# Eight middle taps of a depthwise convolution as products with diagonals on TensorE

## The chip, the cores and the metric

The kernel runs on one core of a Trainium2 chip. The metric is the device time of one execution in microseconds (us). The core has five instruction streams, named here as the profile names them: PE (TensorE; PEld is its weight load), DVE (VectorE), ACT (ScalarE), POOL (GpSimd) and SP (SyncE, which issues the DMA transfers).

## The reference

Two transformer-like blocks run one after the other on 256 tokens of width 1024. The change lies in the first. In each of its two layers half of the channels of the input projection go through a gated convolution over time, the other half through a recurrence (`wkv_scan`) that reads a matrix state. Cut to what matters here:

```python
def conformer_conv(u, conv_w, conv_b, cnorm_g, cnorm_b):
    val, gate = jnp.split(u, 2, axis=-1)
    z = val * jax.nn.sigmoid(gate)
    z = dwconv(z, conv_w) + conv_b          # 31 taps, one filter per channel, 512 channels
    z = group_norm(z, CONV_GROUPS, cnorm_g, cnorm_b, LN_EPS)
    return jax.nn.silu(z)

for l in range(2):
    mod_x = silu(c) @ ada_w[l] + ada_b[l]
    mod_c = silu(c_ctx) @ ada_w[l] + ada_b[l]
...
    yc, s_f, s_b = rwkv_scans(prep_c, s_zero, s_zero, emit=not last)
    prep_x = rwkv_prep(ux[..., CONV_IN:], *rw)
    yx, _, _ = rwkv_scans(prep_x, s_f, s_b, emit=True)
    mix_x = jnp.concatenate([conformer_conv(ux[..., :CONV_IN], *cv), rwkv_out(yx, prep_x, *post)], axis=-1)
    x = x + gt1 * (mix_x @ w_out[l])
    x = x + gt2 * swiglu(modulate(rmsnorm(x, norm2_g[l]), sh2, sc2), ffn_wg[l], ffn_wu[l], ffn_wd[l])
```

There are three such convolutions: on the context in layer 0, on x in layer 0 and on x in layer 1.

## The kernel before, in words

Channels lie on partitions, 128 at a time, and the 256 tokens along the free axis; the 512 channels of a convolution are four feature tiles. The instructions of all stages are written out in Python as generators and then ordered for each engine by a scheduler that follows a modelled timeline, so that the order on an engine isn't the order of the code. Each engine runs its own order strictly in turn.

Two of the convolutions, those of the context in layer 0 and of x in layer 1, run inside `wide` (L1425), the stretches A and B below. `wide` runs the recurrence of that layer (`rwkv`). While that waits, it asks `filler` (L1427) for pieces of other work for TensorE. The filler first gives `conv_in` (L659): per feature tile two weight transfers, the products `pb<-xf,wh` and `pb<-xf,wl`, a sigmoid, and the gate on VectorE (L670), which leaves z in `self.x[0]`. Then it gives `ada_steps` (L478): the modulation vector, as fp32 products of raw weights with 32 columns (`pb<-raw,csil`), in groups of four that lie side by side in TensorE's array, a small product that turns the row (`pb<-const,T2b`), and an addition on VectorE (L503). Almost all products have line L333, the helper `mm`.

The recurrence needs the inverse of small triangular matrices. `inverse` (L944) does it by a recursion of 31 steps on VectorE, a product (L962) and a subtraction (L964) each; the last subtraction is `self.inverted`. Behind it come two 32x32-block transposes on VectorE (L967 into `qt`, L969 into `qc`), products of 32 columns on TensorE, and the writes of the matrix Q on VectorE and ScalarE (the last of them L1011 on VectorE, in the trace as `S<-acc` and `S<-ps` of 32x512). From Q on the sequential `chain` (L1075) can start; its first product is `acc<-Sb,S`. Beside this stand `gram` products whose results VectorE masks (L1029, L1065) and transposes on TensorE (L1035, L1052).

The convolution itself is `conv` (L700). In `wide` its 31 taps are split by their distance from the centre. VectorE takes the centre tap with the bias (L719) and 19 more (L726), each one instruction `T1c += w * z` over a shifted slice. GpSimd takes the 11 outer ones in two instructions each, a product into `tap` (L732) and an addition into the accumulator `acc`, that is `self.x[1]` (L733), which it first sets to zero (L720), and at the end adds VectorE's sum (L737). VectorE's first instruction is tied behind `self.inverted` by `issue_after`, so the taps don't delay the recursion. GpSimd isn't tied. The group norm of `conv` (products `acc<-x,const`) follows, then `mixed_in`.

The third convolution (`hold=True`, x in layer 0) runs on GpSimd alone, in the background of the feed-forward stage. Raw weights pass through a ring of four 512 KB buffers (`raw`, L345), filled by DMAs on SP's queue in the order in which the program asks for them; the filler's products have two PSUM buffers (`pb`).

Of the kernel before, what the change touches and what calls it, by code (L numbers as in the profile page):

```python
# [14 lines left out]
P = 128  # L15
D = 1024
NF = 8
T = 256
# [19 lines left out]
NPOOL, NPOOLE, NPOOLC = (11, 0), (11, 0), (30, 0)  # L38
# [129 lines left out]
def _layout(a):  # L168
# [40 lines left out]
    for l in range(2):  # L209
# [9 lines left out]
        f[f"wo{l}"] = (n["w_out"][l].reshape(NF, P, D))  # L219
        lo = np.zeros((P, 2, 1024), np.float32)  # L220
# [35 lines left out]
EVAC1 = [x for f in range(8) for x in (("DA"[f // 2 % 2 == 0], "e", f), ("A", "h", f), ("P" if f in (4, 5) else "D", "l", f))]  # L256


class Prog:
# [440 lines left out]
    def conv(self, l, z, acc, npool, hold=False):  # L700
# [4 lines left out]
        taps = sorted((j for j in range(31) if j != 15), key=lambda j: abs(j - 15))  # L705
        nv, na = 30 - npool[0] - npool[1], npool[1]
        parts = [("v", taps[:nv]), ("a", taps[nv : nv + na]), ("p", taps[nv + na :])]

        order = []
        for k, js in parts:  # L710
            order += [((i + 0.5) / len(js), k, j) for i, j in enumerate(js)]
        order.sort()
        zc = [acc[:, f, :] for f in range(4)]
        for f in range(4):
            w = lambda j: self.cols[:, o + 4 * j + f : o + 4 * j + f + 1]
            av = self.T1([P, T]) if nv else None
            if nv:
                with self.tc.issue_after(self.inverted.ins):
                    nc.vector.tensor_scalar(av, z[:, f, :], w(15), self.col(f"convb{l}", f), ALU.mult, ALU.add)  # L719
                nc.gpsimd.memset(zc[f], 0.0)  # L720
            else:
                nc.gpsimd.tensor_scalar(zc[f], z[:, f, :], w(15), None, ALU.mult)
            for i, (_, k, j) in enumerate(order):
                d, s = slice(max(0, 15 - j), min(T, T + 15 - j)), slice(max(0, j - 15), min(T, T + j - 15))
                if k == "v":
                    nc.vector.scalar_tensor_tensor(av[:, d], z[:, f, s], w(j), av[:, d], ALU.mult, ALU.add)  # L726
                else:
                    t = self.t(self.pool, [P, T], "tap", bufs=NTAP)
                    if k == "a":
                        nc.scalar.mul(t[:, d], z[:, f, s], w(j))  # L730
                    else:
                        nc.gpsimd.tensor_scalar(t[:, d], z[:, f, s], w(j), None, ALU.mult)  # L732
                    nc.gpsimd.tensor_add(zc[f][:, d], zc[f][:, d], t[:, d])  # L733
                if i % 5 == 4:
                    yield
            if nv:
# [902 lines left out]
```

## Time and profile before

| | us |
|---|---|
| median of 3 runs (lowest, highest) | 2769.9 (2768.45, 2772.62) |
| profiled execution, its own time | 2769.65 |
| its span in the profile | 2767.9 |
| mean granted clock of TensorE | 0.963 |
| busy: TensorE, weight loads | 2618.3, 2278.6 |
| busy: VectorE, ScalarE, GpSimd | 1734.4, 1310.6, 622.5 |
| stretch A, first `wide` (context, layer 0) | about 112 to 316 |
| stretch B, second `wide` (x, layer 1) | about 1107 to 1325 |

Times in the trace are counted from the start of the span. Engines work side by side, so busy times overlap. A granted clock of 1.00 is 2.4 GHz and of 0.50 is 1.2 GHz; a value between them is a mean over a stretch that had both. A row of a timeline groups equal instructions that follow one another; its duration is from the first start to the last end, and the bracket behind it says how long the engine was idle before and what released it.

### The profile page before, as it was taken

How to read it: one execution, taken by the hardware profiler on the slowest of the kernel's cores; microseconds unless marked ns; L12 is line 12 of the kernel's file. 1: busy time of each engine (PE TensorE's matmuls, PEld its weight loads, DVE VectorE, ACT ScalarE, POOL GpSimd, SP SyncE). 2: the span in 40 equal slices, each digit the busy share in tenths (PEclk: the TensorE clock that was granted, in tenths of full speed). 3: DMA queues.
4: the chain of work that ended last, by engine and by line, in shares of the span. 5: the costliest groups of instructions: out<-in, count | busy, mean ns of one | idle time of the engine just before them, and what ended most of it. 6: DMA issues, size and time to landing. Idle time of an engine off the chain costs nothing.

```text
span 2767.9 us, 53680 instructions
## 1 busy us (share of the span) xinstructions
PE 2618.3 (95%) x22398; PEld 2278.6 (82%) x22398; DVE 1734.4 (63%) x2747; ACT 1310.6 (47%) x1984; POOL 622.5 (22%) x609
## 2 busy tenths in 40 slices
PE   7889988999889998899899899999999999999998
PEld 4857867888678897856799899789899898889897
DVE  3895778654577555996555655666655655656655
ACT  5523553434565346423544544644544544644543
POOL 0293999920130001392100000010000000100000
PEclk8989999999999999989999999999999999999999
DMA  7344424434423354253455555524555554525653
GB/s 251 102 153 168 142 97 153 142 127 142 156 77 115 130 180 148 102 184 108 145 184 188 192 187 186 186 77 161 186 186 183 186 187 168 171 77 183 207 188 116
DMA packets 118768, 430.71 MB, mean 156 GB/s; under 512 B 13174, under 2 KB 13686, under 8 KB 118524
## 3 DMA queue, kind: packets, MB, share of 16 engines
q1 hardware_dynamic: 118524, 427.28, 44.6%
q8 instruction: 175, 2.87, 0.4%
q14 instruction: 69, 0.57, 0.1%
HBM read 425.13 MB, written 2.10 MB: 154 GB/s over the span
## 4 chain that ended last, share of the span: by engine, by line
PE 79%; DVE 12%; ACT 5%; issue 2%; DMA 2%; POOL 1%; SPq 0%; ACTq 0%; DVEq 0%; POOLq 0%
PE pb L333 33%; PE acc L333 25%; PE ps L333 19%; DVE wl L342 3%; DVE T L962 1%; DVE S L964 1%; DMA raw<-in_ada 1%; ACT wh L341 1%; PE acc L438 0%; DVE acc L619 0%; ACT L384 0%; DVE T1c L726 0%; DVE x L620 0%; DMA raw<-in_wr 0%; DVE S L1029 0%
## 5 line engine op out<-in xcount | busy, mean ns | idle before, releaser
L342 DVE TENSOR_TENSOR wl<-raw,wh 128x1024 fp32r<-128x1024 f32 (+1 forms) x654 | 812.8, 1246 | 618.6 <-ACT wh L341 388.1
L341 ACT CAST wh<-raw 128x1024 fp32r<-128x1024 f32 (+1 forms) x654 | 682.3, 1046 | 918.4 <-PE pb L333 356.6
L333 PE MATMUL pb<-xf,wh 128*128 128x256 f32 (+1 forms) x2560 | 490.1, 289 | 12.1 <-ACT T1b L585 4.2
L333 PE MATMUL pb<-S,wh 128*128 128x256 f32 x2560 | 493.2, 289 | 7.3 <-DVE wa L630 3.4
L333 PEld LDWEIGHTS pb<-xf,wh 128*128 128x128 f32 (+1 forms) x2560 | 409.3, 193 | 27.7 <-DVE T1b L588 4.9
L333 PEld LDWEIGHTS pb<-S,wh 128*128 128x128 f32 x2560 | 409.8, 193 | 24.4 <-issue 10.2
L333 PE MATMUL ps<-S,wh 128*128 128x256 f32 x2048 | 390.5, 287 | 1.9 <-ACT S L460 1.0
L333 PE MATMUL pb<-xf,wl 128*128 128x256 f32 (+1 forms) x1280 | 368.9, 289 | 2.6 <-DVE wl L342 2.5
L333 PE MATMUL pb<-S,wl 128*128 128x256 f32 x1280 | 368.2, 288 | 1.6 <-DVE wl L342 1.6
L365 POOL TENSOR_TENSOR wl<-raw,wh 128x1024 fp32r<-128x1024 f32 x22 | 52.0, 2375 | 1404.4 <-ACT wh L364 964.0
L333 PEld LDWEIGHTS ps<-S,wh 128*128 128x128 f32 x2048 | 326.4, 192 | 11.5 <-issue 3.7
L333 PE MATMUL ps<-S,wl 128*128 128x256 f32 x1024 | 293.2, 286 | 0.1
L333 PEld LDWEIGHTS pb<-xf,wl 128*128 128x128 f32 (+1 forms) x1280 | 247.3, 193 | 8.8 <-DVE wl L342 4.7
L333 PEld LDWEIGHTS pb<-S,wl 128*128 128x128 f32 x1280 | 246.3, 192 | 5.8 <-issue 3.1
L333 PE MATMUL acc<-wh,T 128*128 128x512 f32 x704 | 206.2, 393 | 0.0
L333 PEld LDWEIGHTS ps<-S,wl 128*128 128x128 f32 x1024 | 196.1, 192 | 2.4 <-issue 1.5
L333 PE MATMUL acc<-wh,T1b 128*128 128x512 f32 x528 | 158.7, 400 | 3.5 <-ACT T1b L341 3.5
L333 PEld LDWEIGHTS acc<-wh,T 128*128 128x128 f32 x704 | 127.0, 189 | 23.7
L732 POOL TENSOR_SCALAR tap<-z,cols 128x255 f32<-128x255 f32 (+14 forms) x120 | 145.3, 1220 | 0.0
L333 PEld LDWEIGHTS acc<-wh,T1b 128*128 128x128 f32 x528 | 95.7, 191 | 22.4 <-ACT T1b L341 4.4
L333 PE MATMUL acc<-wl,T 128*128 128x512 f32 x352 | 113.0, 395 | 0.0
L733 POOL TENSOR_TENSOR z<-z,tap 128x255 f32<-128x255 f32 (+14 forms) x120 | 112.0, 933 | 4.1
(444 smaller groups left out, 3907.4 us busy)
## 6 DMA issues: line engine op xcount, KB each, us to landing
raw<-in_fu SPq DMA_DIRECT2D x132, 512.0 KB, 3.2
raw<-in_ada SPq DMA_DIRECT2D x96, 512.0 KB, 4.0
raw<-in_pu SPq DMA_DIRECT2D x88, 512.0 KB, 4.3
raw<-in_qu SPq DMA_DIRECT2D x88, 512.0 KB, 4.2
raw<-in_fd SPq DMA_DIRECT2D x66, 512.0 KB, 3.2
raw<-in_wr SPq DMA_DIRECT2D x51, 512.0 KB, 3.3
raw<-in_pd SPq DMA_DIRECT2D x44, 512.0 KB, 4.2
raw<-in_qd SPq DMA_DIRECT2D x44, 512.0 KB, 4.2
```

The source lines that it names most:

```text
L333: return self.nc.tensor.matmul(out, lhsT, rhs, start=start, stop=stop, **kw)
L341: self.nc.scalar.copy(hi, src)
L342: self.nc.vector.tensor_sub(lo, src, hi.bitcast(F32))
L365: self.nc.gpsimd.tensor_sub(lo, r, hi.bitcast(F32))
L732: nc.gpsimd.tensor_scalar(t[:, d], z[:, f, s], w(j), None, ALU.mult)
L733: nc.gpsimd.tensor_add(zc[f][:, d], zc[f][:, d], t[:, d])
L962: nc.vector.tensor_mul(tv, tj[:, k + 1 : 32, k : k + 1].broadcast_to([P, m, k + 1]), X[:, k : k + 1, 0 : k + 1].broadcast_to([P, m, k + 1]))
L964: self.inverted = nc.vector.tensor_sub(X[:, k + 1 : 32, 0 : k + 1], X[:, k + 1 : 32, 0 : k + 1], tv)
```

## The change

The taps are sorted by their distance from the centre (`TAPS`). The eight middle ones, the centre included, become products on TensorE: for each of them and each feature tile the host lays out a 128x128 matrix that has the tap's 128 weights on its diagonal (`cd0`, `cd1`; eight matrices of a tile in one array of 512 KB). The new `conv_first` loads these and multiplies them in fp32 with the shifted slices of z, summed in one PSUM buffer, and ScalarE writes the sum with the bias into `acc`. It stands in the filler between `conv_in` and `ada_steps`. VectorE keeps 12 taps per tile and first sets its sum to zero; GpSimd keeps its 11 taps and adds them to what ScalarE wrote. In the third convolution GpSimd's first instruction takes the bias along, so that the last one goes. The second `wide` uses `cd1`, the first `cd0`. Lines of the new file lie 10 to 12 further down.

```diff
--- before.py
+++ after.py
@@ -35,7 +35,8 @@
 
 NLAST = 2, 4
 
-NPOOL, NPOOLE, NPOOLC = (11, 0), (11, 0), (30, 0)
+TAPS = sorted(range(31), key=lambda j: abs(j - 15))
+NTENS, NPOOL = 8, 11
 NTAP = 2
 
 QB, QE, QC, EVERY = (2, 3, 4, 5), (2, 3, 4, 5), (1,), 2
@@ -217,6 +218,12 @@
         uc = _up(w[:, :D])
         f[f"wc{l}"] = (np.stack([uc[:4], uc[4:]], 1).reshape(8, P, D))
         f[f"wo{l}"] = (n["w_out"][l].reshape(NF, P, D))
+
+        cw, cd = n["conv_w"][l].reshape(31, 4, P), np.zeros((4, P, NTENS, P), np.float32)
+        for i in range(NTENS):
+            for p in range(4):
+                cd[p, np.arange(P), i, np.arange(P)] = cw[TAPS[i], p]
+        f[f"cd{l}"] = cd.reshape(4, P, NTENS * P)
         lo = np.zeros((P, 2, 1024), np.float32)
         lo[:64, 0] = n["decay_up"][l].transpose(1, 0, 2).reshape(64, 1024)
         lo[64, 0] = n["decay_b0"][l].reshape(1024)
@@ -254,6 +261,11 @@
     "A h 5,P l 5,A h 6,A h 7,D l 6,D l 7").split(",")]
 EVAC = [(e, op, int(f)) for e, op, f in EVAC]
 EVAC1 = [x for f in range(8) for x in (("DA"[f // 2 % 2 == 0], "e", f), ("A", "h", f), ("P" if f in (4, 5) else "D", "l", f))]
+
+
+def tap(j):
+
+    return slice(max(0, 15 - j), min(T, T + 15 - j)), slice(max(0, j - 15), min(T, T + j - 15))
 
 
 class Prog:
@@ -697,46 +709,44 @@
             self.split(src, *mix[f])
         return mix
 
-    def conv(self, l, z, acc, npool, hold=False):
+    def conv_first(self, l, z, acc):
+
+        for f in range(4):
+            r = self.raw(f"cd{l}", f)
+            pc = self.ps((P, T))
+            for i, j in enumerate(TAPS[:NTENS]):
+                d, s = tap(j)
+                self.mm(pc[:, d], r[:, i * P : i * P + P], z[:, f, s], i == 0, i == NTENS - 1)
+            self.nc.scalar.activation(acc[:, f, :], pc, AF.Identity, bias=self.col(f"convb{l}", f))
+            yield
+
+    def conv(self, l, z, acc, hold=False):
 
 
         nc = self.nc
         o = COLS[f"convw{l}"][0]
-        taps = sorted((j for j in range(31) if j != 15), key=lambda j: abs(j - 15))
-        nv, na = 30 - npool[0] - npool[1], npool[1]
-        parts = [("v", taps[:nv]), ("a", taps[nv : nv + na]), ("p", taps[nv + na :])]
-
-        order = []
-        for k, js in parts:
-            order += [((i + 0.5) / len(js), k, j) for i, j in enumerate(js)]
-        order.sort()
+        n = 31 if hold else NPOOL
         zc = [acc[:, f, :] for f in range(4)]
         for f in range(4):
             w = lambda j: self.cols[:, o + 4 * j + f : o + 4 * j + f + 1]
-            av = self.T1([P, T]) if nv else None
-            if nv:
+            if hold:
+                nc.gpsimd.tensor_scalar(zc[f], z[:, f, :], w(15), self.col(f"convb{l}", f), ALU.mult, ALU.add)
+            else:
+                av = self.T1([P, T])
                 with self.tc.issue_after(self.inverted.ins):
-                    nc.vector.tensor_scalar(av, z[:, f, :], w(15), self.col(f"convb{l}", f), ALU.mult, ALU.add)
-                nc.gpsimd.memset(zc[f], 0.0)
-            else:
-                nc.gpsimd.tensor_scalar(zc[f], z[:, f, :], w(15), None, ALU.mult)
-            for i, (_, k, j) in enumerate(order):
-                d, s = slice(max(0, 15 - j), min(T, T + 15 - j)), slice(max(0, j - 15), min(T, T + j - 15))
-                if k == "v":
+                    nc.vector.memset(av, 0.0)
+                for j in TAPS[NTENS : 31 - n]:
+                    d, s = tap(j)
                     nc.vector.scalar_tensor_tensor(av[:, d], z[:, f, s], w(j), av[:, d], ALU.mult, ALU.add)
-                else:
-                    t = self.t(self.pool, [P, T], "tap", bufs=NTAP)
-                    if k == "a":
-                        nc.scalar.mul(t[:, d], z[:, f, s], w(j))
-                    else:
-                        nc.gpsimd.tensor_scalar(t[:, d], z[:, f, s], w(j), None, ALU.mult)
-                    nc.gpsimd.tensor_add(zc[f][:, d], zc[f][:, d], t[:, d])
+            for i, j in enumerate(TAPS[1:] if hold else TAPS[31 - n :]):
+                d, s = tap(j)
+                t = self.t(self.pool, [P, T], "tap", bufs=NTAP)
+                nc.gpsimd.tensor_scalar(t[:, d], z[:, f, s], w(j), None, ALU.mult)
+                nc.gpsimd.tensor_add(zc[f][:, d], zc[f][:, d], t[:, d])
                 if i % 5 == 4:
                     yield
-            if nv:
+            if not hold:
                 nc.gpsimd.tensor_add(zc[f], zc[f], av)
-            else:
-                nc.gpsimd.tensor_scalar(zc[f], zc[f], self.col(f"convb{l}", f), None, ALU.add)
             yield
         while hold and not self.go:
             yield
@@ -1426,7 +1436,8 @@
 
             def filler():
 
-                steps = itertools.chain(self.conv_in(l, x, fl(self.x[0])), self.ada_steps(l, ada))
+                steps = itertools.chain(self.conv_in(l, x, fl(self.x[0])),
+                                        self.conv_first(l, fl(self.x[0]), fl(self.x[1])), self.ada_steps(l, ada))
 
                 def fill(n=1):
                     lane = self.lane
@@ -1442,7 +1453,7 @@
                 if at == "post" and before is not None:
                     before()
             self.on("c")
-            drain(self.conv(l, fl(self.x[0]), fl(self.x[1]), (NPOOL, NPOOLE)[l]))
+            drain(self.conv(l, fl(self.x[0]), fl(self.x[1])))
             self.pstags = beside
             self.on("b")
             return self.mixed_in(fl(self.x[1]), self.y, perm)
@@ -1480,7 +1491,7 @@
         self.on("b")
         acc = z()
         self.go = False
-        self.bg = self.conv(0, zx, acc, NPOOLC, True)
+        self.bg = self.conv(0, zx, acc, True)
         self.mods, self.every = self.ada_steps(1, QC), EVERY
         self.ffn_add(0, self.x, 1, f)
         drain(self.mods)
```

**TensorE in stretch A**, from the last product of `conv_in` (`pb_2105`) to the inverse's 32-column products (`ps_1715<-S_1711`). `raw,csil` and `T2b` are the modulation, `const,S_496` the transposes of L1035, `S_1098,S_496` a gram product. Before:

```order
L333 MATMUL pb_2105<-xf_242,wl_2102 128x256
L333 MATMUL pb_2157<-raw_2158,csil 32x512 x2
L333 MATMUL pb_2157<-raw_2162,csil 32x512 x2
L333 MATMUL pb_2157<-raw_2166,csil 32x512
...
L333 MATMUL pb_2176<-const,T2b_2174 128x2 x4
L333 MATMUL pb_2215<-raw_2216,csil 32x512 x2
L1035 MATMUL acc_239_1489<-const,S_496 128x128 x4
L333 MATMUL pb_2215<-raw_2220,csil 32x512 x2
L1035 MATMUL acc_240_1495<-const,S_496 128x128 x4
...
L333 MATMUL ps_1715<-S_1711,S_883 32x32 x31
```

And with the change, the same place (`x_67,raw` are the products with diagonals, `pb_2159`, `pb_2171`, `pb_2216` and `pb_2228` the four feature tiles):

```order
L345 MATMUL pb_2105<-xf_242,wl_2102 128x256
L345 MATMUL pb_2159<-x_67,raw_2157 128x256
L345 MATMUL pb_2159<-x_67,raw_2157 128x255 x2
...
L345 MATMUL pb_2171<-x_67,raw_2169 128x252
L1045 MATMUL acc_239_1489<-const,S_496 128x128 x4
L1045 MATMUL acc_240_1495<-const,S_496 128x128 x4
L345 MATMUL pb_2216<-x_67,raw_2214 128x256
...
L345 MATMUL pb_2228<-x_67,raw_2226 128x255
L1062 MATMUL acc_244_1504<-const,S_299 64x128 x4
L345 MATMUL acc_245_1511<-S_885,S_493 64x64 x4
L345 MATMUL ps_1715<-S_1711,S_883 32x32 x32
```

The products with diagonals stand where modulation products stood; the first modulation product now comes behind the last product with a diagonal, which stands behind the 32-column products.

**VectorE in stretch A**, from the recursion's last subtraction (`S_1189<-S_1189,T_208`) to the first transpose. L719 and L726 are the conv's taps. Before:

```order
L964 TENSOR_TENSOR S_1189<-S_1189,T_208_1282 128x31
L719 TENSOR_SCALAR T1c_2875<-x_67,cols 128x256
...
L726 SCALAR_TENSOR_TENSOR T1c_2987<-x_67,cols,T1c_2987 128x255
L1029 TENSOR_TENSOR S_1447<-acc_236_1468,const 128x256
L1029 TENSOR_TENSOR S_1447<-acc_237_1469,const 128x256
L726 SCALAR_TENSOR_TENSOR T1c_3043<-x_67,cols,T1c_3043 128x255
...
L726 SCALAR_TENSOR_TENSOR T1c_2931<-x_67,cols,T1c_2931 128x254
L967 STREAM_TRANSPOSE S_1711<-S_1189 128x1024
```

With the change (L737 sets the sums to zero, L740 are the taps, L1039 and L977 are L1029 and L967 of before):

```order
L974 TENSOR_TENSOR S_1189<-S_1189,T_208_1282 128x31
L737 MEMSET T1c_2923 128x256
...
L740 SCALAR_TENSOR_TENSOR T1c_2923<-x_67,cols,T1c_2923 128x252
L1039 TENSOR_TENSOR S_1447<-acc_236_1468,const 128x256
L1039 TENSOR_TENSOR S_1447<-acc_237_1469,const 128x256
L740 SCALAR_TENSOR_TENSOR T1c_2971<-x_67,cols,T1c_2971 128x252
...
L740 SCALAR_TENSOR_TENSOR T1c_3067<-x_67,cols,T1c_3067 128x250
L977 STREAM_TRANSPOSE S_1711<-S_1189 128x1024
```

Four first taps became four memsets, and L1039 stands behind one tap instead of three.

**VectorE in stretch A, behind the second transpose**, up to the writes of Q (L1011, now L1021). Before (L1065 masks, L987 and L995 prepare Q):

```order
L969 STREAM_TRANSPOSE S_1713<-S_1189 128x1024
L726 SCALAR_TENSOR_TENSOR T1c_2987<-x_67,cols,T1c_2987 128x252
...
L987 MEMSET S_1785 128x1024
...
L995 COPY S_1786<-S_1713 32x16x32 x2
L1065 TENSOR_TENSOR T_255_1572<-acc_254_1563,const 64x256
L726 SCALAR_TENSOR_TENSOR T1c_2987<-x_67,cols,T1c_2987 128x250
L1011 TENSOR_SCALAR S_1785<-acc_285_1788 32x16x32
```

With the change:

```order
L979 STREAM_TRANSPOSE S_1713<-S_1189 128x1024
L740 SCALAR_TENSOR_TENSOR T1c_2923<-x_67,cols,T1c_2923 128x246
...
L997 MEMSET S_1785 128x1024
...
L1005 COPY S_1786<-S_1713 32x16x32 x2
L1075 TENSOR_TENSOR T_255_1572<-acc_254_1563,const 64x256
L1075 TENSOR_TENSOR T_258_1585<-acc_256_1575,const 64x256
L1021 TENSOR_SCALAR S_1785<-acc_285_1788 32x16x32
```

Of the taps four stand directly behind the transpose, and all others ahead of it; between the preparation and the writes of Q, and behind these, there are none.

## Rows read from the trace of the kernel before

**Rows 1.** Page, busy time and share of the span of each engine.

```profile
PE 2618.3 (95%) x22398; PEld 2278.6 (82%) x22398; DVE 1734.4 (63%) x2747; ACT 1310.6 (47%) x1984; POOL 622.5 (22%) x609
```

**Rows 2.** Page, the chain that ended last, share of the span by engine.

```profile
PE 79%; DVE 12%; ACT 5%; issue 2%; DMA 2%; POOL 1%; SPq 0%; ACTq 0%; DVEq 0%; POOLq 0%
```

**Rows 3.** Windows: length, busy us of PE, PEld, DVE, ACT, POOL, granted clock, DMA share, GB/s.

```profile
132.00:160.00 28.00, 26.81 (x337) 23.39 (x338) 27.35 (x50) 7.78 (x12) 25.09 (x25) 1.00 0.33 116
160.00:168.00 8.00, 2.83 (x18) 1.11 (x12) 7.76 (x18) 0.59 (x1) 7.84 (x10) 0.85 0.77 290
168.00:188.00 20.00, 19.62 (x232) 11.96 (x232) 19.26 (x41) 4.55 (x8) 19.61 (x19) 0.72 0.35 119
188.00:216.00 28.00, 23.42 (x265) 14.01 (x266) 27.43 (x54) 8.99 (x13) 23.80 (x23) 0.65 0.48 180
216.00:302.00 86.00, 84.70 (x1042) 63.19 (x1039) 44.47 (x93) 34.78 (x63) 41.52 (x50) 1.00 0.40 142
1144.00:1188.00 44.00, 40.46 (x484) 36.01 (x483) 41.19 (x82) 15.61 (x25) 23.79 (x23) 1.00 0.29 103
1188.00:1200.00 12.00, 7.28 (x59) 2.91 (x58) 11.72 (x26) 1.17 (x2) 11.77 (x15) 0.71 0.61 221
1200.00:1216.00 16.00, 16.00 (x196) 9.47 (x195) 15.08 (x32) 2.80 (x5) 15.69 (x15) 0.71 0.34 113
1216.00:1244.00 28.00, 27.29 (x374) 17.49 (x377) 23.31 (x43) 11.04 (x16) 27.60 (x27) 0.87 0.67 243
1244.00:1288.00 44.00, 42.32 (x770) 31.71 (x765) 32.38 (x82) 12.34 (x24) 14.54 (x15) 1.00 0.51 178
```

**Rows 4.** Timeline of PE, stretch A: start, us, engine, line, operation [idle before <-releaser].

```profile
162.75 1.02 PE L333 MATMUL pb<-const,T2b 128*128 128x2 f32 x8 [1.92 <-DVE x L670]
...
168.31 1.11 PE L1035 MATMUL acc<-const,S 128*128 128x128 f32 x4 [3.56 <-DVE S L1029]
```

**Rows 5.** Timeline of PE, stretch B: group norm of conv, then the stretch's end.

```profile
1291.61 0.60 PE L333 MATMUL acc<-x,const 128*128 128x256 f32 x2
1292.04 1.03 PE L333 MATMUL acc<-S,const 128*128 128x256 f32 x4
...
1306.25 1.22 PE L333 MATMUL acc<-rks,const 128*128 128x256 f32 x2
1307.27 2.21 PE L333 MATMUL acc<-gl,S 128*128 128x256 f32 x4
```

**Rows 6.** Timeline of PE, stretch A: modulation products, four and eight together.

```profile
223.47 1.05 PE L333 MATMUL pb<-raw,csil 128*32 128x512 f32 x4
...
227.69 1.06 PE L333 MATMUL pb<-raw,csil 128*32 128x512 f32 x8
```

**Rows 7.** Timeline of DVE, stretch A: two steps of the recursion.

```profile
131.74 0.39 DVE L962 TENSOR_TENSOR T<-S,S 128x231 f32<-128x231 f32 x1
...
150.34 0.80 DVE L962 TENSOR_TENSOR T<-S,S 128x231 f32<-128x231 f32 x1
```

**Rows 8.** Timeline of DVE, stretch A: taps, second transpose, last write of Q.

```profile
163.82 2.50 DVE L719 TENSOR_SCALAR T1c<-x,cols 128x256 f32<-128x256 f32 x4
...
187.31 1.96 DVE L969 STREAM_TRANSPOSE S<-S 128x1024 f32<-128x1024 f32 x1
...
206.27 0.68 DVE L1011 TENSOR_SCALAR S<-ps 32x512 f32<-32x512 f32 x1
...
211.95 6.26 DVE L726 SCALAR_TENSOR_TENSOR T1c<-x,cols,T1c 128x248 f32<-128x248 f32 x16
```

**Rows 9.** Timeline of POOL: first tap in A and B, last addition in B.

```profile
134.52 1.88 POOL L732 TENSOR_SCALAR tap<-x,cols 128x246 f32<-128x246 f32 x2 [24.30 <-DVE x L670]
...
1163.81 1.98 POOL L732 TENSOR_SCALAR tap<-x,cols 128x246 f32<-128x246 f32 x2 [22.55 <-DVE x L670]
...
1270.27 0.73 POOL L737 TENSOR_TENSOR x<-x,T1c 128x256 f32<-128x256 f32 x1
```

**Rows 10.** Groups by line: ScalarE's evictions of the same shape.

```profile
L628 ACT ACTIVATE S<-pb,cols 128x256 f32<-128x256 f32 x28 | 13.1, 470 | 0.0
```

## The prediction

> **What bounds the kernel now.** I first read the engines' shares of the page, because they say where added work hurts: TensorE is busy for 95% of the span and VectorE for 63% [rows 1]. I then read the chain that ended last: 79% of it is TensorE and 12% VectorE [rows 2]. So the kernel is TensorE's work, with places where it waits for VectorE. The change touches two places, the two calls of `wide`: stretch A (112 to 316 us) and stretch B (1107 to 1325 us). I cut these into stages, where the reader is to see busy time, idle time and granted clock side by side [rows 3]. While VectorE runs the recursion of `inverse` (132 to 160 us in A, 1144 to 1188 us in B), TensorE has its `conv_in` products and hardly idles. From 160 and from 1188 us on it idles 5.17 and 4.72 us within 8 and 12 us. After that it is busy again, but the granted clock has a mean of 0.72 and 0.65 in A and of 0.71 in B: more than half of that time it is at the lower of its two levels (1.2 GHz). From 216 and from 1244 us on it is at 1.00 again. All this while VectorE is busy: 54.45 of 56 us in A, 50.1 of 56 in B. What TensorE waits for in the hole can be read from its timeline: 1.92 us for the gated z, then 3.56 us for a VectorE result of L1029 [rows 4].
>
> A change that adds TensorE work therefore costs its full price, except for what falls into those holes, and what it gives back by keeping the clock at its upper level (2.4 GHz).
>
> **What is added on TensorE.** Per stretch there are 4 x 8 = 32 fp32 products with 128 columns of weights and 252 to 256 of data, two instructions each. The nearest rows are the group-norm products of the same shape: one that starts at 1291.61 is followed by the next at 1292.04, so 0.43 us each; at the lower clock, from 1306.25 to 1307.27, it is 1.02 us [rows 5]. I take 0.43, since the products are dense and stand where `conv_in` ends, at clock 1.00: 64 x 0.43 = **+27.5 us**. The upper bound, all at the lower clock, is 64 x 1.02 = 65.3 us.
>
> The modulation products (`pb<-raw,csil`, 32 columns) move back. Eight of them that stand together take 1.06 us, four alone 1.05 us [rows 6]: neighbours run side by side. Counted in the order of the instructions, they need 24 such time slots in A and 25 in B before, and 26 and 26 now, because more of them stand alone: 3 x 1.05 = **+3.2 us**.
>
> **What is given back on TensorE.** (1) The hole behind the inverse. The products of the first two feature tiles need only z and their diagonals, so they fill it: 5.17 + 4.72 = **-9.9 us**.
> (2) The lower clock right behind the hole. The loss of a stage is its busy time by what the clock lacks [rows 3]: 2.83 x 0.15 + 19.62 x 0.28 in A and 7.28 x 0.29 + 16.00 x 0.29 in B, 0.4 + 5.5 + 2.1 + 4.6 = **-12.6 us**. I take it whole: in the rows it follows the hole, and the hole is now filled.
> (3) The lower clock further on, 23.42 x 0.35 + 27.29 x 0.13 = 11.7 us: I take none. It follows later waits, in the middle of the inverse's and the chain's own products, which the change leaves in place.
> (4) Idle time in the same two stages, 28.00 - 23.42 and 28.00 - 27.29 = 5.3 us: waits for VectorE, whose taps grow fewer. I take half, **-2.6 us**.
> (5) Idle time beside the recursion, 1.19 + 3.54 = 4.7 us. GpSimd's taps now wait for the first eviction, so they no longer run beside the recursion. A step of it that took 0.39 us before GpSimd started took 0.80 us beside GpSimd [rows 7]. VectorE's recursion will be shorter by some microseconds, but TensorE has only this idle time to turn into a gain. I take half, **-2.4 us**.
>
> **VectorE.** Its taps fall from 20 to 12 per feature tile: per stretch 4 x 0.62 + 28 x 0.39 = 13.4 us go [rows 8], and four memsets come. Between the recursion and the first transpose (L967, now L977) there are now 4 memsets, 16 taps and two others, where 14 taps and three others stood: that transpose comes no sooner by counting. Between the second transpose at 187.31 us and the last write of Q at 206.27 us [rows 8] stood 20 taps in A, and stand 4 now, 16 x 0.39 = 6.2 us. So the chain can start about 6 us sooner per stretch. This is no term of its own: TensorE then has the modulation products still to do which it had done before, and they fill `chain`, a stage where it is 98% busy. What I count of it is the idle time in (4).
>
> **GpSimd, ScalarE, queues.** GpSimd keeps its 11 taps, loses four memsets per stretch, and its first add waits for the eviction of the first tile. Before it starts at 134.52 and 1163.81 us, in the new kernel some 30 us later, at about 165 and 1192 us. In B it ended at 1270.27 us [rows 9]; 28 us later is 1299, past the first group-norm product at 1291.61 [rows 5]. But in the stages from 1144 to 1244 it was busy 23.79 + 11.77 + 15.69 + 27.60 us, and in the 27 us after them 14.54 us, the only work of its there [rows 3]: 93.4 us of work, which from 1192 us ends at about 1285. I count it at nothing, by a margin of 6 us; if that cover goes, each us late costs one. The eight evictions on ScalarE cost 8 x 0.47 us [rows 10] beside a ScalarE that is busy for under half of each stage: nothing, and no row speaks for more than those 3.8 us. The eight transfers of 512 KB stand on SP's queue behind those of `conv_in` and ahead of `ada`, which they delay. The DMA share is 0.34 to 0.77 behind the hole [rows 3], and products that are delayed with them have later stages to run in: nothing; at worst the hole stays open, 9.9 us. The fused bias of the third conv removes four GpSimd instructions in the background of the FFN: nothing, below or above.
>
> **The sum.** 27.5 + 3.2 - 9.9 - 12.6 - 2.6 - 2.4 = +3.2 us on the profiled execution's 2769.65 us, 2772.85, say **2773 us**. That execution lies 0.25 us under the median of the runs, so no correction is made. About 0.2%, 5.5 us, is what a measurement of this kernel can tell from no change, so this is "no change", a little on the slow side.
>
> **A rule that bears on it.** The rows say that TensorE is busy for 98% to 100% of the stages from 168 to 188 us and from 1200 to 1216 us. The Trainium skill, page "Perfetto Trace Analysis", section "Identifying the Most-Contended Engine", says that matmul busy time is a poor measure of the headroom and that the busy share of the weight loads is a better one. By it the stage from 168 to 188 us, at 11.96 of 20, would have 8 us of room, and the sum would be that of the first rival. The trace here has both readings, and that the clock was low there explains the same gap, so I don't follow it beyond (2).
>
> **The rivals.**
> First, *VectorE holds the chain*: it is 97% busy in A, and after the chain's start another 26 taps stand between the chain's own instructions. Then with fewer taps the chain runs ahead, the modulation products fall into stages at clock 1.00, and the rest of the idle time and of the lower clock goes too: up to 2.7 + 2.3 + 11.7 = 16.7 us, 2756; with three quarters of it 2760.5, about **2760 us: faster**. For it speaks VectorE's share; against it that TensorE is busy for 19.62 of 20 us in A and 16.00 of 16 in B behind the hole [rows 3], so that it is not VectorE alone that holds the stage. 0.30.
> Second, *the clock stays low* (the other side): the products of the third and fourth tile stand behind the `acc<-const,S` products, which wait for VectorE's L1029 as in [rows 4]. If that wait stays a hole, the clock falls in it as before, (2) is lost and the products behind pay more: 2773 + 12.6 = **2786 us**; with half of those 32 products at 1.02 us, 9.4 more, 2795. It decides if more than half of that wait of 3.56 us stays. For it: L1029 still has 4 memsets and a tap ahead of it on VectorE; against it: before it had four first taps and three more ahead. 0.16.
> Third, *GpSimd is late*: if its instructions take as long in calendar time as before, the group norm in B waits 1299 - 1291.6 = 7.4 us: **2780 us**. 0.08.
> That the change doesn't do what it says, because VectorE's saved time is spent ahead of the first transpose on taps drawn forward, would take (4) and (5) away: 2778. 0.02.
>
> **How the numbers follow.** The forecast's case, 2767 to 2779, has what is left, 0.44. Faster by over 0.2% is the first rival, 0.30. Within 0.2% (2764.4 to 2775.4) is the forecast's case without its upper edge, which I put at 0.07: 0.37. Slower is that edge with the other rivals, 0.07 + 0.16 + 0.08 + 0.02 = 0.33. The range reaches down to 2757, where the first rival has its whole 16.7 us but one, and up to 2787, just past the second; what lies beyond (products at the lower clock, an open hole, other moves of the schedule) I put at 0.2. Since cases of both signs have weight: the likeliest one alone has the range 2767 to 2779.
>
> **What would show it.** Right: a product row of 0.43 us each with the granted clock at 1.00 from 160 to 175 us; no idle time above 1 us there; the last Q write about 6 us nearer to the second transpose; recursion steps at 0.4 us; GpSimd's last conv add in B before 1292 plus what B is shifted. Wrong on the fast side: clock at 1.00 through the start of the chain. Wrong on the slow side: an idle row at L1045 of some microseconds with the clock at 0.50 behind it, or the group norm's product waiting for GpSimd.

## The result, and the profile after

The changed kernel takes 2798.65 us (median of 5 runs, 2795.52 to 2803.29) where the kernel before took 2769.0 (5 runs): a ratio of 1.0108, 95% interval 1.0094 to 1.0123. It is some 30 us slower. A second set of five beside other runs gave 2801.22 us and 1.0128 (1.0106 to 1.0150). The profiled execution took 2803.29 us, its span is 2801.5 us.

The page's busy times answer to [rows 1] and the shares of the chain that ended last to [rows 2]:

```profile
PE 2653.6 (95%) x22526; PEld 2309.1 (82%) x22526; DVE 1691.9 (60%) x2691; ACT 1317.6 (47%) x1994; POOL 597.0 (21%) x597
...
PE 77%; DVE 9%; ACT 4%; POOL 3%; DMA 3%; issue 2%; SPq 0%; ACTq 0%; DVEq 0%; POOLq 0%
```

TensorE has 35.3 us more, VectorE 42.5 us less, and TensorE's share of the span is the same 95%. In the chain VectorE fell from 12% to 9%, and GpSimd and DMA rose from 1% and 2% to 3% each: something that waits for GpSimd now lies on the chain. In stretch B its rows (start, us) run from GpSimd's taps to modulation transfers:

```profile
1218.50 7.19 POOL tap L744 x2
1227.20 4.93 POOL tap L744 x2
1280.21 4.19 DMA raw<-in_ada
```

The windows of stretch A and B, with the columns of [rows 3]:

```profile
160.00:175.00 15.00, 12.04 (x184) 10.69 (x183) 15.00 (x26) 3.04 (x6) 14.69 (x18) 0.86 0.20 73
175.00:200.00 25.00, 21.87 (x274) 15.73 (x269) 20.45 (x38) 9.19 (x13) 22.99 (x22) 0.77 0.37 127
200.00:220.00 20.00, 20.00 (x295) 12.63 (x296) 5.79 (x15) 5.82 (x12) 19.53 (x26) 0.88 0.52 181
220.00:240.00 20.00, 17.86 (x213) 9.44 (x208) 3.25 (x9) 2.90 (x7) 18.88 (x25) 1.00 0.54 190
240.00:260.00 20.00, 18.02 (x211) 9.99 (x211) 3.91 (x11) 2.30 (x5) 0.00 (x0) 0.91 0.79 290
...
1200.00:1240.00 40.00, 37.37 (x501) 29.13 (x503) 36.59 (x69) 12.32 (x19) 39.45 (x36) 0.78 0.27 95
1240.00:1260.00 20.00, 20.00 (x239) 11.26 (x231) 5.92 (x15) 4.46 (x9) 19.53 (x26) 0.94 0.54 189
1260.00:1280.00 20.00, 18.54 (x265) 10.83 (x263) 4.80 (x13) 4.23 (x9) 19.61 (x26) 1.00 0.50 182
1280.00:1300.00 20.00, 15.15 (x126) 6.81 (x128) 2.21 (x7) 1.92 (x4) 1.84 (x3) 0.74 0.72 262
```

VectorE is nearly free from 200 us on (5.79, 3.25, 3.91 of 20). But TensorE now idles from 220 to 260 and from 1260 to 1300 us, where it was nearly full before up to 1288 [rows 3], and from 1280 to 1300 the clock's mean is 0.74. The timeline of TensorE says what it waits for there:

```profile
154.53 5.83 PE L345 MATMUL pb<-x,raw 128*128 128x254 f32 x26
160.20 1.04 PE L1045 MATMUL acc<-const,S 128*128 128x128 f32 x8
...
172.83 2.47 PE L345 MATMUL acc<-S,S 64*64 64x64 f32 x50 [2.96 <-DVE T L1075]
175.23 3.99 PE L345 MATMUL pb<-x,raw 128*128 128x255 f32 x12
...
241.97 1.47 PE L345 MATMUL pb<-raw,csil 128*32 128x512 f32 x4 [3.59 <-DMA raw<-in_ada]
...
1213.11 1.11 PE L345 MATMUL acc<-S,S 64*64 64x64 f32 x8 [2.63 <-DVE T L1075]
...
1284.45 1.92 PE L345 MATMUL pb<-raw,csil 128*32 128x512 f32 x4 [5.71 <-DMA raw<-in_ada]
```

Most products with diagonals cost what was forecast: 13 of them take 5.83 us, 0.45 each. The last six of A stand behind a wait, with a mean clock of 0.77 in that window, and take 3.99 us, 0.66 each. The hole of [rows 4] is gone. The new waits are for VectorE's L1075, 2.96 and 2.63 us, and for modulation transfers, 3.59 and 5.71 us. SP's timeline (start, us, what it issues) and its waits (us in total, times, longest) show why the modulation transfers came late:

```profile
237.14 0.33 SPq L1535 DMA_DIRECT2D x<-in_ctx  x1
237.56 16.64 SPq L360 DMA_DIRECT2D raw<-in_ada  x10
...
1253.19 15.53 SPq L360 DMA_DIRECT2D raw<-in_ada  x9
1279.80 0.33 SPq L1516 DMA_DIRECT2D x<-keep  x1
1280.21 18.99 SPq L360 DMA_DIRECT2D raw<-in_ada  x11
```

```profile
SPq L1535 <- POOL tap L744: 6.4, 1, 6.4
...
SPq L1516 <- POOL tap L744: 11.0, 1, 11.0
```

A transfer that refills the buffer in which z lies (`x<-in_ctx`, `x<-keep`) has moved up among the modulation transfers. It must wait until GpSimd has read z for its last tap, 6.4 and 11.0 us, and ten and eleven modulation transfers stand behind it. In the kernel before it stood behind all of them.

To see where the time went I split TensorE's time in both stretches, between the same ScalarE instructions in every trace, into work at full clock (busy by granted clock), idle time, and busy time lost to the clock, summed over windows of 4 us. All numbers are us; "lost" is idle and clock of both stretches together, and the last column is the ratio of the runs' times to those of the kernel before, measured beside them. The rows below "changed, again" are the experiments of the next section; "tied" means that a refill is held behind the last modulation transfer.

```
                              A work idle clock    B work idle clock   lost A+B   ratio
before                         185.0 19.2 19.0     235.9 27.8 17.9      83.9      1
changed                        201.5 17.6 13.1     251.1 27.7 23.8      82.2      1.0108
changed, again                 199.4 17.8 16.3     252.4 27.2 23.6      84.9      1.0128
refill on GpSimd's queue       201.0 13.3 11.9     249.9 22.3 16.1      63.6      1.0068
sum into VectorE's tile        203.3 11.8  6.3     254.3 23.3 17.9      59.3      1.0049
both of these                  201.5 11.0 11.0     248.0 30.1 24.4      76.5      1.0070
before, refill on that queue   185.7 19.0 16.7     230.2 36.2 29.5     101.4      1.0054
refill tied in B               199.7 17.1 14.5     250.7 23.8 16.5      71.9      1.0096
refill tied in B, again        198.8 17.1 17.9     250.1 23.6 25.7      84.3      1.0125
refill tied in A and B         200.8 14.0 11.0     246.5 23.6 21.9      70.5      1.0054
  and sum in VectorE's tile    202.5 14.0 11.1     250.8 25.1 26.4      76.6      1.0078
one product, tied A and B      184.6  9.2 13.0     233.9 28.7 23.3      74.2      0.9953
before, 13 taps, tied          183.0 17.8 20.9     232.6 25.9 21.1      85.7      1.0011
before, GpSimd late, tied      180.6 12.7 26.9     233.6 22.3 12.6      74.5      0.9941
two products, tied A and B     188.2 10.0 22.9     236.6 31.9 24.9      89.7      1.0045
four products, tied A and B    191.5 10.3 17.5     238.9 21.9 27.3      77.0      1.0030
sixteen, tied A and B          215.6 10.8 11.0     262.9 22.4 17.3      61.5      1.0126
```

The work grew by 16.5 and 15.2 us, 31.7 together; 27.5 for the products and 3.2 for the modulation products, 30.7, were forecast. The lost time was to shrink by the terms (1), (2), (4) and (5), which also come to 27.5; it went from 83.9 to 82.2 and stands elsewhere. Outside the two stretches the profiled run took another 4 us: 7 in the stages from 460 to 790 us, where the schedule came out differently, less 3 elsewhere. The split of a single profile has its own spread: the same program gave 71.9 and 84.3 us of lost time, nearly all of the difference in the clock.

### The profile page after: what moved, and what is told of

It is laid out like the page before. It is cut to its first block, busy times and chain, and to the rows that moved or that the text cites. A ratio compares the mean times of both kernels' runs of the same rounds, so it can differ in the third digit from the quotient of the medians.

```text
span 2801.5 us, 53920 instructions
## 1 busy us (share of the span) xinstructions
PE 2653.6 (95%) x22526; PEld 2309.1 (82%) x22526; DVE 1691.9 (60%) x2691; ACT 1317.6 (47%) x1994; POOL 597.0 (21%) x597
## 4 chain that ended last, share of the span: by engine, by line
PE 77%; DVE 9%; ACT 4%; POOL 3%; DMA 3%; issue 2%; SPq 0%; ACTq 0%; DVEq 0%; POOLq 0%
PE pb L345 32%; PE acc L345 24%; PE ps L345 19%; DMA raw<-in_ada 2%; POOL tap L744 2%; DVE wl L354 2%; POOL x L745 1%; DVE T1c L740 1%; ACT wh L353 1%; DVE S L861 0%; PE acc L450 0%; DVE acc L631 0%; DMA raw<-in_wr 0%; ACT L396 0%; DVE x L632 0%
```

## The experiments

Theory 1 was the held queue, Theory 2 that TensorE's products are paid in full whatever stands around them. Theory 3, from the fifth run on, was that the order which the scheduler makes around an edit moves the time.

**The refill on another queue, GpSimd early again, both, and the kernel before with the other queue.** The edits, in this order (the third has both, the fourth is the first edit in the kernel before):

```diff
-        self.load("ctx", self.x)
+        for b in range(2):
+            nc.gpsimd.dma_start(self.x[b], self.ap["ctx"][b * P : b * P + P, :])
-            nc.sync.dma_start(self.x[b], self.keep[b])
+            nc.gpsimd.dma_start(self.x[b], self.keep[b])
```

```diff
-            self.nc.scalar.activation(acc[:, f, :], pc, AF.Identity, bias=...)
+            av = self.lt("T1", [P, T], lane="c")
+            self.nc.scalar.activation(av, pc, AF.Identity, bias=...)
+            self.avs.append(av)
...
-                av = self.T1([P, T])
-                with self.tc.issue_after(self.inverted.ins):
-                    nc.vector.memset(av, 0.0)
+                av = self.avs[f]
+                nc.gpsimd.memset(zc[f], 0.0)
```

> The changed kernel with one edit: the refill of the buffers in which z and the accumulator lie (x<-in_ctx behind stretch A, x<-keep behind stretch B) is issued from GpSimd's queue and no longer stands on SP's queue among the modulation transfers. Theory 1 (held queue): the refill waits for GpSimd's last tap, 6.4 us in A and 11.0 us in B, and 10 or 11 modulation transfers stand behind it; with the refill elsewhere SP runs on, at least these 17 us come back and perhaps the lower clock behind them, so 2768 to 2782 us. Theory 2 (price of the products): TensorE has 27.5 us of new products and the time is theirs; the transfers only seem late because the products came first; 2793 to 2803 us.

> The changed kernel, but ScalarE writes the eight-tap sum into VectorE's tile T1c, where VectorE adds its 12 taps, and GpSimd clears its accumulator itself as before the change, so that its taps can start beside the recursion again, some 25 us sooner. The refill stays on SP's queue. Theory 1 (held queue): GpSimd is done some 10 to 25 us sooner, the refill no longer waits, 2770 to 2785 us, with the recursion some 6 us longer per stretch. Theory 2 (price of the products): the same TensorE work, 2793 to 2806 us.

> Both edits of the last two runs together. Theory 1: when the queue is free GpSimd's end matters only for the group norm, so within 5 us of the better of the two. Theory 2: 2793 to 2806 us.

> The kernel before the change with the refills on GpSimd's queue alone. Theory 1: the refill held nothing up there (0.4 us in B, none in A), so no gain: 2764 to 2775 us. A gain of over 10 us here would mean that the other queue is worth something by itself and that the first run doesn't speak for Theory 1. Theory 2: 2764 to 2775 us as well.

Measured, beside 2766.57 us for the kernel before: 2786.98 (1.0068, 1.0049 to 1.0087), 2782.24 (1.0049, 1.0030 to 1.0068), 2787.09 (1.0070, 1.0049 to 1.0092) and 2782.71 (1.0054, 1.0038 to 1.0070). The first lies between the two theories. The second lies inside the range of Theory 1, and the third within the 5 us of the second that Theory 1 gave it; all three are faster than Theory 2 said. The first two give back a third to a half of the 30 us. But the fourth is a miss of the experiment's design. The kernel before should not have changed and got 16 us slower: by the traces the scheduler put the instructions of stretch B in another order, and its lost time rose from 45.7 to 65.7 us. Order and GpSimd's queue can't be told apart in it. So such an edit alone can move the time by 15 us, and the first run can't be read as the price of the queue.

**The same refill, tied behind the last modulation transfer.** In B alone, in A and B, and in A and B with ScalarE's sum in VectorE's tile:

```diff
+            with self.tc.issue_after(self.lastraw["ada"].ins):
-            nc.sync.dma_start(self.x[b], self.keep[b])
+                nc.sync.dma_start(self.x[b], self.keep[b])
```

The tie in B changes exactly one row of SP's order and none of the other four engines.

> The changed kernel in which the refill behind stretch B (x<-keep, one transfer on SP) is tied behind the last modulation transfer. The orders of TensorE, VectorE, ScalarE and GpSimd are those of the changed kernel, instruction by instruction; on SP one transfer stands 11 places later, where it stands in the kernel before. Theory 1 (held queue): the 11.0 us wait goes and with it the stall and the lower clock behind it, 10 to 25 us: 2774 to 2789 us, and up to the refill the trace of B is unchanged. Theory 2 (price of the products): 2793 to 2803 us. Theory 3 (the schedule around the edit, not the queue, made the first run's gain): no schedule moves here, so 2793 to 2803 us.

> The same tie in both stretches (the refill x<-in_ctx behind A as well). Here the scheduler moves other instructions behind A too. Theory 1: A gives back its 6.4 us wait and some of the clock on top of B: 2764 to 2783 us. Theory 2 and 3: 2790 to 2803 us.

> Both ties, and ScalarE's sum goes into VectorE's tile, so that GpSimd starts beside the recursion again. Theory 1: with the queue free GpSimd's end no longer holds a transfer, so within 8 us of the run with both ties alone, in either direction. If GpSimd's late start has a cost of its own, by the group norm that waits for it, this run is faster by more than that. Theory 2: 2790 to 2806 us.

Measured, beside 2768.58 us: 2794.1 (1.0096, 1.0059 to 1.0134), 2783.1 (1.0054, 1.0035 to 1.0074) and 2793.0 (1.0078, 1.0055 to 1.0102). The tie in B took the stall away, but no measurable time, which is the range of Theories 2 and 3. Both ties together end at the edge of Theory 1's range. GpSimd early again made the kernel with both ties slower by the medians, not faster; the two intervals overlap. The kernel with the tie in B was timed again, beside the changed kernel.

> The changed kernel itself, timed beside the next one on the same chip: 2793 to 2803 us by every theory, 1.0094 to 1.0123 of the kernel before.

> The changed kernel with one transfer of SP's order moved 11 places back (the refill behind stretch B), once more with more rounds. Theory 1 (held queue): the profile of the first run shows stretch B 10.4 us shorter than in the changed kernel (290.1 against 300.5), so 8 to 13 us less than the changed kernel in the same call. Theory 2 (price of the products) and Theory 3 (schedule around the edit): within 3 us of it.

Measured, beside 2764.61 us: 2801.22 us (1.0128, 1.0106 to 1.0150) and 2799.34 us (1.0125, 1.0102 to 1.0148), no difference. SP's timeline and the windows of the second run with the tie in B, and below them one window of the first:

```profile
1257.00 35.65 SPq L362 DMA_DIRECT2D raw<-in_ada  x20
1292.75 0.38 SPq L1519 DMA_DIRECT2D x<-keep  x1
```

```profile
1240.00:1260.00 20.00, 20.00 (x221) 12.05 (x222) 5.17 (x14) 4.50 (x9) 19.53 (x27) 0.75 0.46 161
1260.00:1280.00 20.00, 19.56 (x265) 11.11 (x265) 5.30 (x13) 3.84 (x8) 19.61 (x26) 1.00 0.75 258
1280.00:1300.00 20.00, 19.60 (x231) 10.04 (x233) 3.65 (x11) 2.30 (x5) 2.73 (x4) 1.00 0.85 305
```

```profile
1240.00:1260.00 20.00, 20.00 (x276) 12.21 (x272) 5.11 (x13) 5.04 (x10) 19.53 (x26) 0.98 0.62 211
```

The 20 transfers run through, and TensorE is busy for 19.60 us from 1280 to 1300 where it was for 15.15. But the clock stands at 0.75 from 1240 to 1260, where the changed kernel had 0.94 and the first run of this same program 0.98. The idle time went (27.2 to 23.6 us in B), and the clock took it back in that run and not in the other. So the held queue in B is real as a stall, and its worth in time isn't shown. With both ties the kernel is 0.5 to 0.7% faster than the changed one, and stretch A is 225.8 us long instead of 232 to 233: there the tie also moved other instructions, so queue and schedule can't be told apart.

**The products and the relief, each by itself.** One product per tile in place of eight (on the kernel with both ties), and VectorE's taps cut to 13 in the kernel before (with both ties, too, which the cut of the edit leaves out):

```diff
-            for i, j in enumerate(TAPS[:NTENS]):
+            for i, j in enumerate(TAPS[:1]):
...
-        parts = [("v", taps[:nv]), ("a", taps[nv : nv + na]), ("p", taps[nv + na :])]
+        parts = [("v", taps[7:nv] if nv else []), ("a", taps[nv : nv + na]), ("p", taps[nv + na :])]
```

> The kernel with both ties, with one product with a diagonal per feature tile in place of eight; seven of the eight middle taps are left out of the result, VectorE keeps its 12 taps, the transfers of the diagonals stay. 56 products of 0.43 us go, 24.1 us of TensorE work. Theory 1 in its full form (the products lie in the holes and the rest of the loss was the queue): 3 to 10 us less than with both ties, 2773 to 2780 us. Theory 2 (TensorE pays the products nearly in full): 18 to 26 us less, 2757 to 2765 us, under the kernel before.

> The kernel before with both refills tied, and VectorE's taps cut from 20 to 13 per feature tile without any product in their place; seven taps are left out of the result, GpSimd starts beside the recursion as before. It shows what the relief of VectorE is worth by itself. The forecast's terms for it (idle time behind the recursion, half the later waits) would give some 5 to 15 us, 2754 to 2764 us; if TensorE's own work is the bound behind the hole, under 5 us, 2764 to 2771 us.

Measured, beside 2764.61 us: 2752.37 (0.9953, 0.9933 to 0.9972) and 2766.57 (1.0011, 0.9995 to 1.0027). The first lies under the ranges of both theories, on the side of Theory 2. Between eight products (1.0054) and one lie 1.0% of the time, 28 us, for 24.1 us of products by the forecast's price and 28.8 us of work by the split. The run with 7 of 20 taps less and no product in their place shows no gain; its lost time is 85.7 us against 83.9. But its trace has TensorE's and VectorE's instructions in another order than the kernel before, so a gain that the order took back isn't excluded.

**GpSimd late without products, and other numbers of products.** In the kernel before, GpSimd's accumulator is cleared from the finished inverse, so that its additions wait for the recursion; then, in the changed kernel, `NTENS` 2 and 4 (VectorE takes the other taps, 18 and 16 per tile), and each of the eight products twice. All four have both ties, which the cuts leave out:

```diff
-                nc.gpsimd.memset(zc[f], 0.0)
+                nc.gpsimd.tensor_scalar(zc[f], self.inv[:, 768:1024], 0.0, None, ALU.mult)
...
-NTENS, NPOOL = 8, 11
+NTENS, NPOOL = 2, 11
```

> The kernel before (no products) with both refills tied, in which GpSimd's accumulator is cleared by a product of the finished inverse with zero, so that GpSimd's additions start only behind the recursion, as in the changed kernel. It shows what GpSimd's later start is worth by itself. If the run with one product owes its 12 us below the kernel before to it (the recursion beside GpSimd takes 27.6 us of VectorE time in each stretch, some 6 us of it by contention): 2752 to 2762 us. If TensorE's work is all that counts: 2761 to 2770 us. If GpSimd's later end holds the group norm: 2768 to 2780 us.

> Both ties, and two taps per tile on TensorE, 18 on VectorE, the whole result. Theory 2 (each product is paid in full, 64 x 0.43 = 27.5 us for eight, 3.4 us per tap): with eight taps 14.5 us over the kernel before, so with two 14.5 - 20.6 = -6 us: 2755 to 2762 us. Theory 1: the products lie in holes, fewer of them leave holes open: 2768 to 2783 us.

> Both ties, and four taps per tile on TensorE, 16 on VectorE. Theory 2: 14.5 - 13.8 = +1 us over the kernel before, 2761 to 2770 us. Theory 1: 2768 to 2783 us.

> Both ties, and each of the eight products issued twice (sixteen per tile into the same sum, which changes the result). Theory 2: 14.5 + 27.5 = 42 us over the kernel before, 2800 to 2812 us. Theory 1: the holes are full by now, so the second eight are paid in full by this theory too; the difference of the theories lies in the runs with fewer.

Measured, beside 2768.97 us: 2753.5 (0.9941, 0.9925 to 0.9956), 2783.31 (1.0045, 1.0030 to 1.0060), 2773.78 (1.0030, 1.0016 to 1.0045) and 2804.63 (1.0126, 1.0109 to 1.0143).

TensorE's work in A lies on a line, 184.6, 188.2, 191.5, 200.8 and 215.6 us for 1, 2, 4, 8 and 16 products per tile: 2.1 us per product and stretch, above the 4 x 0.43 = 1.7 us of its own. The times don't. Two products (1.0045) are no faster than four (1.0030) or, nearly, than eight (1.0054), though eight have 22.5 us more of work in the two stretches than two; the kernels with two and four lie within or just past the range of Theory 1, and some 20 and 4 us above the ranges of Theory 2. From eight to sixteen the work grows by 31.2 us and the time by some 20, while the lost time falls from 70.5 to 61.5 us. So the straight line that Theory 2 expected holds for the work and not for the time. The orders differ between all of these kernels.

The run with GpSimd late is 15 us faster than the kernel before and leaves nothing out; it beats both kernels. In its trace TensorE, VectorE and ScalarE run their instructions in the order of the kernel before, but for neighbours that changed places, and on SP only `x<-in_ctx` stands later, behind weight transfers. So this gain, unlike most here, is not one of the order: it belongs to GpSimd's later start, with that one refill moved. Its recursion on VectorE, the view of one line (durations in ns: least, median, most; first and last start), first of the kernel before, then of this one:

```profile
L962 DVE TENSOR_TENSOR T<-S,S x31: 189/407/1012, 114.7 to 163.5; 128x31 f32<-128x31 f32 x2, 128x60 f32<-128x60 f32 x2, 128x87 f32<-128x87 f32 x2, 128x112 f32<-128x112 f32 x2
```

```profile
L965 DVE TENSOR_TENSOR T<-S,S x31: 193/351/566, 110.4 to 151.1; 128x31 f32<-128x31 f32 x2, 128x60 f32<-128x60 f32 x2, 128x87 f32<-128x87 f32 x2, 128x112 f32<-128x112 f32 x2
```

The recursion took 48.8 us from its first to its last product and takes 40.7 us; in B it is 45.1 and 37.7. On GpSimd and VectorE of that run:

```profile
151.70 3.47 POOL L722 TENSOR_SCALAR x<-S 128x256 f32<-128x256 f32 x4 [20.22 <-DVE S L967]
```

```profile
174.35 1.92 DVE L972 STREAM_TRANSPOSE S<-S 128x1024 f32<-128x1024 f32 x1
...
192.67 0.68 DVE L1014 TENSOR_SCALAR S<-ps 32x512 f32<-32x512 f32 x1
```

GpSimd's additions wait until 151.70 us, where in the kernel before its taps ran from 134.52 us on [rows 9], and the last write of Q is 13.6 us sooner than in [rows 8]. The Trainium skill, page "SBUF — State Buffer", section "Who interferes with whom", says that VectorE and GpSimd share a port pair under an exclusive lock. The trace agrees in that the steps beside GpSimd took up to 1.01 us and without it none took over 0.57; a lock as such isn't seen in it.

Most of it lies in B, where work, idle time and clock fall from 281.6 to 268.5 us together. In A, where Q is ready 13.6 us sooner, they fall only from 223.2 to 220.2, as the loss to the clock rises from 19.0 to 26.9 us. Beside products the same step was worth less: GpSimd late against early is 1.0054 against 1.0078 with both ties and 1.0068 against 1.0070 with the refills on GpSimd's queue, in orders that differ.

## Why the prediction was wrong

Forecast was 2773 us, within 2757 to 2787, as no change; measured 2798.65.

- **The added work: right.** 30.7 us were forecast, the split shows 31.7, and the products cost 0.45 us each at the upper clock. It doesn't tell the products from the modulation products. Eight against one product differ by 28 us, in another order.
- **The holes and the clock, terms (1) and (2): this step failed.** "The hole is now filled" is true of the old hole: TensorE has no idle row from 152 to 169 us. But the next opens behind it, 2.96 us up to 172.83 us, and the clock of the window from 175 us on is 0.77. "I take it whole" was wrong. The lost time of both stretches stayed at 82.2 to 84.9 us where 83.9 less 27.5 was forecast. In A it fell by 4 to 8 us; in B it rose by 5 to 6, with a wait of 2.63 us for VectorE's L1075, one of 5.71 us for a modulation transfer, and the clock at 0.78 from 1200 to 1240 and at 0.74 from 1280 to 1300 us. I had treated idle and slow time as a supply that new work uses up. In the changed kernel it formed again behind the new work. That it must isn't shown: with the same products, and the refills or ScalarE's sum placed otherwise, it was 59.3 to 76.6 us in all runs but those with the tie in B alone (71.9 and 84.3). So part of the credit was there to be had, in another order; which cause holds how much of it is open.
- **The relief of VectorE, term (4): not seen.** The run with 13 taps and no products shows no gain, in an order of its own. In the changed kernel the second transpose and the last write of Q stand 17.3 us apart (19.0 before), not 12 to 13. VectorE's timeline there:

```profile
183.46 1.92 DVE L979 STREAM_TRANSPOSE S<-S 128x1024 f32<-128x1024 f32 x1
...
194.82 0.67 DVE L1021 TENSOR_SCALAR S<-acc 32x512 f32<-32x512 f32 x1
...
200.76 0.68 DVE L1021 TENSOR_SCALAR S<-ps 32x512 f32<-32x512 f32 x1 [4.58 <-PE ps L345]
```

  VectorE now waits 4.58 us for TensorE, in whose order products with diagonals and modulation products stand ahead. So what the taps save there is spent on waiting.

- **GpSimd beside the recursion, term (5): the sign right, the size wrong.** I gave 2.4 us, because TensorE had little idle time beside the recursion. In the kernel before, GpSimd late is worth 15 us, most of it in B: Q and the chain behind the recursion come sooner as well. The recursion is shorter in the changed kernel too (41.0 us in A, 36.6 in B, as against 48.8 and 45.1 before); how much of the 15 us is in its time isn't shown.
- **GpSimd's end and the queues: "nothing" was wrong as a stall.** The third rival had the right cause, GpSimd's later end, in the wrong place: its last addition in B was at 1281.27 us and the group norm's first product only at 1321.59, without a wait:

```profile
1281.27 0.72 POOL L749 TENSOR_TENSOR x<-x,T1c 128x256 f32<-128x256 f32 x1
```

```profile
1321.59 0.70 PE L345 MATMUL acc<-x,const 128*128 128x256 f32 x2
```

  It was the refill of z's buffer, on SP's queue, that waited for GpSimd. I had counted the eight new transfers and not looked at which old transfer waits for GpSimd and what stands behind it. With the ties 3 to 4 us of idle time go in each stretch, in A together with a change of order; how many us of the end the held queue costs is open.
- **The second rival** ("the clock stays low") was nearest in time, 2786 us. Its place was wrong, since L1045 doesn't wait in the new trace; its result, (2) not coming in, was right. That its number came nearest is luck.
- The rule of the Trainium skill that I weighed (page "Perfetto Trace Analysis", section "Identifying the Most-Contended Engine") would have had 8 us of room from 168 to 188 us. No run tests that stage alone. The changed kernel didn't use any such room; from eight to sixteen products some 11 of 31 us of work cost no time, in another order, and the split doesn't say where.

What stays open is the size of single causes beyond the work. All edits but two, the tie in B and GpSimd late, made the scheduler order the rest anew, and kernels that should have been equal differ by up to 16 us. The sum of the separate runs, GpSimd late -15, eight products +28, queue and schedule (both ties undone) +15 to +20, comes to 28 to 33, about what was measured. But these runs are steps of one way from the kernel before to the changed one, with only the 3 us from GpSimd late to one product left out, so their sum has to come out near it, whatever each step consists of. An order held fixed for all of these edits wasn't tried.

## What to carry to other kernels

Work that is moved onto the engine that bounds the kernel comes as full work (31.7 us here). The idle and slow stretches that it would fill are no sure credit: of the 27.5 us that I took, 1.7 came. Where the order of instructions is made by a scheduler, compare the orders of two kernels first, and read a single cause only from runs that keep the order. When an engine is made to finish later, look for transfers that refill what it reads and for what stands behind them on their queue. And before work is moved to another engine, try to move it in time: two engines that slow each other gave 15 us here by a later start of one, with the work left as it was.

## What the runs showed of the hardware that I had not expected

The mean granted clock of the same program (the kernel with the tie in B) in the same stretch differed from run to run, 0.98 and 0.75 from 1240 to 1260 us, with TensorE busy for 20.00 of 20 us in both. The time lost to the clock in B was 16.5 and 25.7 us. Lost time of a stretch read from one profile is thus uncertain by some 10 us, while the idle time in it repeated to 0.2 us (17.1 and 17.1, 23.8 and 23.6), and to 0.5 in the two profiles of the changed kernel.
